# Inputs and outputs of a streaming-encoder layer laid out around the launch, with a new order at the start

## The chip, the cores and the metric

The kernel runs on one core of a Trainium2 chip, in one launch. The metric is the device time of that launch in microseconds (us). What the host does before the launch and after it (here: reshaping and transposing arrays) is no part of it.

## The reference, cut to what matters

One layer, for 1024 prompt rows and 32 sample rows (the sample has 256 cached keys and 30 rows of convolution state). Everything is float32.

```
mod = silu(c) @ w_ada + b_ada;  shift, scale, gate = split(mod, 3)
h = rms_norm(x, g_norm) * (1 + scale) + shift
q, k, v, gate_a, iq, iw, ik, glu, gate_b, merge = split(h @ w_in)
k_all, v_all, ik_all = concat([past_k, k]), concat([past_v, v]), concat([past_ik, ik])
score = sum over 8 heads of iw * relu(iq . ik_all / 8)      # the indexer
idx = top_k(score, 256 of 1024 keys; 72 of 288 for the sample)
o = softmax(q . k_all[idx] / sqrt(128)) @ v_all[idx];  y_a = (o * silu(gate_a)) @ w_a
u = ga * sigmoid(gb);  u_ext = concat([conv_state, u])
dw = depthwise conv of u_ext, width 31, + b_dw;  n = layer_norm(dw, g_ln, b_ln)
y_b = (silu(n) * silu(gate_b)) @ w_b
x = x + gate * ((sigmoid(m_a) * y_a + sigmoid(m_b) * y_b) @ w_out);  y = rms_norm(x, g_final)
outputs: y, k, v, ik and u_ext[-30:], each for the prompt and for the sample
```

## The kernel before, in words

Activations live channel by row: a tile has 128 channels on its partitions and the 1056 rows (1024 and 32) along its free axis. A matrix product in float32 is three passes of float32r: operands are split into a high and a low part, and `mm3` (lines 132 to 134) or `proj` (line 563) multiplies high by high, high by low and low by high. `proj` takes eight steps of 128 input channels; in a step it issues nine matmuls of 352 columns, and after each step it calls `step`, which takes one entry from the list `side` (transposes, indexer dots) and some convolution operations for VectorE. So whatever stands in `side` is laid between the steps of the big projections, on the same TensorE queue.

The program has a start and a long main part. The start ends when the first full projection begins. It loads the nine row tiles of x (`x:0` to `x:8`, the last being the sample; 512 KB each, six buffers), the first two thirds of `w_ada` in eight blocks of 1 MB (`a:g,h` is column group g, input half h; three buffers), the 72 columns of `w_in` for the index keys (`k`), and two blocks of 128 columns for the index queries (`q:0`, `q:1`). The loads are written in the table `LOADS` and go through SyncE's queue in that order. What the engines do with them is written in the table `ORDER`, one word per step:

- `sq`, `v`, `s`, `r`, `x`: square, variance, root, reciprocal and scaling of a row tile (the letter behind `x:i` names the engine, D VectorE, P GpSimd, A ScalarE); `t:i,h` four TensorE transposes of half a row tile into PSUM (two PSUM buffers), `c:i,h` the copy of them into `xT`.
- `m:g,h` four matmuls of `silu(c)` with a block of `w_ada`; `a:g`, `o:g`, `O:g` bring the sum of a column group into channel-by-row form and add the bias. A group serves two of the eight channel blocks.
- `h`, `i`, `l`, `S`: modulated h, its high part, its low part, and the sample's rows. Of a channel block, part `f` is rows 0 to 255, `i` 256 to 767, `t` 768 to 1023, `tf` both outer parts.
- `q:k,c` and `k:k,c`: three matmuls of channel block k for the index queries (512 or 288 columns) and index keys (352 columns). `wa`, `wd` split a weight; `b` transposes and `B` finishes the bias; `z:n` issues n matmuls on zeros that fill TensorE.

TensorE, VectorE and ScalarE run in the order written; GpSimd's queue and SyncE's after `LOADS` are ordered by the compiler. An engine waits for the instruction at the head of its queue.

In the main part the kernel transposes on TensorE what comes from the host by row and is needed by channel, or the other way: `vecs` (convolution weights, biases and state), `cache_ik` and `cache_kT` (cached keys), `nat` (k and v, which the host wants by row) and `conv_out` (the last 30 rows of u).

Of the kernel before, what the change touches and what calls it, by code (L numbers as in the profile page):

```python
# [79 lines left out]
""")  # L80
ORDER = steps("""
sq:8 z:3 b s:8 v:8 r:8 sq:3 x:8,P v:3 s:3 B sq:4 r:3 z:4 t:8,1 t:8,0 x:3,P c:8,1,D s:4 v:4 sq:5 r:4 x:4,D c:8,0,A v:5
s:5 z:4 t:4,1 r:5 t:4,0 c:4,1,A x:5,P c:4,0,D t:3,0 m:0,0 c:3,0,A sq:2 t:5,0 t:3,1 v:2 s:2 c:3,1,A r:2 c:5,0,A z:1
m:0,1 x:2,P wa:k t:5,1 a:0,D wd:k,P t:2,0 c:5,1,D sq:6 c:2,0,D z:1 t:2,1 o:0 s:6 v:6 sq:7 r:6 c:2,1,D x:6,P s:7 v:7
r:7 O:0 z:5 t:6,0 x:7,P c:6,0,A h:i,1,D z:1 m:1,0 S:0,D i:i,1 h:i,0,P i:i,0 l:i,1 t:7,0 t:7,1 c:7,0,A l:i,0 k:1,1
i:t,0 h:t,0,P c:7,1,D m:1,1 i:t,1 h:t,1,P l:t,0 k:0,1 a:1,D wa:0 k:0,2 l:t,1 o:1 wd:0,D t:6,1 sq:0 k:1,2 q:0,1 s:0
v:0 q:0,0 c:6,1,A r:0 q:1,0 O:1 x:0,P h:i,3,D i:i,2 m:2,0 h:i,2,D S:1,P i:i,3 l:i,2 t:0,0 sq:1 t:0,1 k:2,1 c:0,1,D
q:2,0 s:1 v:1 c:0,0,A r:1 q:1,1 x:1,D l:i,3 m:2,1 t:1,0 a:2,A t:1,1 c:1,0,D q:3,0 c:1,1,A h:f,0,D h:f,1,P i:tf,2
h:tf,2,D k:3,1 h:tf,3,D m:3,0 i:f,1 l:tf,2 i:tf,3 o:2 l:f,1 k:2,0 O:2 i:f,0 q:2,1 l:tf,3 i:i,4 S:2,P k:1,0 m:3,1
l:f,0 i:tf,4 h:tf,5,D i:tf,5 h:i,4,D q:3,1 h:i,5,P k:3,0 l:i,4 a:3,A k:3,2 h:tf,4,D i:i,5 k:0,0 l:tf,4 q:4,0 wa:1  # L90
l:i,5 o:3 k:4,2 O:3 k:4,0 l:tf,5 i:i,7 S:3,P q:4,1 k:5,1 h:i,7,D i:i,6 q:5,0 l:i,7 i:tf,6 k:5,2 h:i,6,D h:tf,6,P
q:5,1 i:tf,7 l:i,6 k:5,0 q:7,0 h:tf,7,P l:tf,6 k:7,1 wd:1,P q:6,0 l:tf,7 k:6,2 q:6,1 q:7,1 k:7,2 k:7,0 k:6,1 k:2,2
k:4,1 k:6,0
# [1682 lines left out]
```

## Time and profile before

| | us |
|---|---|
| median of 3 runs (1257.99 to 1259.17) | 1259.0 |
| the profiled execution | 1258.4 |
| its span, first to last instruction | 1256.6 |
| TensorE busy in the span | 1236.4 (98%) |
| VectorE, ScalarE, GpSimd busy | 894.0, 610.4, 181.4 |

The profiled execution took 1.8 us more than its span; sums are made against it. It agrees with the median to 0.6 us. Busy time of TensorE is modelled from pipelined matmuls, so a matmul's own duration (0.27 us for a small one) is longer than the time by which it holds up the next. What an instruction costs is read from the distance between starts.

### The profile page before, as it was taken

The numbers are of one execution on the slowest core, as the hardware profiler recorded it, in microseconds if no ns is written. First come the engines' busy times: TensorE is split into PE (matmuls) and PEld (weight loads), VectorE is DVE, ScalarE is ACT, GpSimd is POOL, SyncE is SP. The second block draws the span as 40 slices with busy tenths as digits, with TensorE's granted clock in tenths as the row PEclk, the third lists the DMA queues.
The fourth block names the chain that finished last, engine by engine and source line by source line (L and its number), as shares of the span: only waits on it lengthen the run. The fifth ranks groups of instructions, "written<-read, shape, count | busy, mean of one in ns | idle before, by whom it ended". The sixth has DMA issues, their size and how long they took to land.

```text
span 1256.6 us, 19134 instructions
## 1 busy us (share of the span) xinstructions
PE 1236.4 (98%) x7453; PEld 1171.9 (93%) x7453; DVE 894.0 (71%) x1416; ACT 610.4 (49%) x1128; POOL 181.4 (14%) x285
## 2 busy tenths in 40 slices
...
GB/s 314 221 51 69 73 98 59 78 69 70 102 53 53 101 52 88 67 69 78 100 98 103 171 104 47 92 203 244 39 88 89 91 105 193 207 152 180 161 88 85
DMA packets 116396, 138.49 MB, mean 110 GB/s; under 512 B 10523, under 2 KB 97843, under 8 KB 116176
## 3 DMA queue, kind: packets, MB, share of 16 engines
...
q8 instruction: 59, 0.97, 0.3%
q14 instruction: 33, 0.27, 0.1%
...
## 4 chain that ended last, share of the span: by engine, by line
PE 96%; DMA 1%; DVE 1%; ACT 1%; SPq 0%; issue 0%; POOL 0%; POOLq 0%
PE proj L563 70%; PE PT L1302 2%; PE y L132 2%; PE y L134 2%; PE y L133 2%; PE O L132 1%; PE O L134 1%; PE O L133 1%; PE misc L761 1%; PE misc L762 1%; PE misc L134 1%; PE misc L133 1%; PE misc L132 1%; DMA ada<-in_w_ada_dram 1%; PE proj L132 1%; PE proj L134 1%
## 5 line engine op out<-in xcount | busy, mean ns | idle before, releaser
L985 DVE SCALAR_TENSOR_TENSOR s<-u,vec,s 128x1086 f32<-128x1086 f32 x240 | 314.5, 1347 | 2.8
L563 PE MATMUL proj<-hh,wh 128*128 128x352 f32 x1440 | 312.1, 325 | 0.0
L563 PE MATMUL proj<-hl,wh 128*128 128x352 f32 x1440 | 311.5, 324 | 0.0
L563 PE MATMUL proj<-hh,wl 128*128 128x352 f32 x1440 | 309.1, 323 | 0.0
L563 PEld LDWEIGHTS proj<-hh,wh 128*128 128x128 f32 x1440 | 244.4, 188 | 1.8
L563 PEld LDWEIGHTS proj<-hh,wl 128*128 128x128 f32 x1440 | 246.0, 188 | 0.0
L563 PEld LDWEIGHTS proj<-hl,wh 128*128 128x128 f32 x1440 | 244.9, 188 | 0.0
L831 ACT ACTIVATE relu<-scores,cand 128x384 bf16<-128x384 f32 (+6 forms) x224 | 183.6, 821 | 72.5 <-DVE cand L846 69.9
L129 DVE TENSOR_TENSOR wl<-raw,wh 128x1024 fp32r<-128x1024 f32 (+1 forms) x82 | 97.9, 1196 | 72.1 <-ACT wh L128 72.0
L128 ACT CAST wh<-raw 128x1024 fp32r<-128x1024 f32 (+1 forms) x82 | 83.8, 1024 | 56.7 <-PE proj L563 44.6
L775 DVE SCALAR_TENSOR_TENSOR scores<-relu,iws,scores 128x384 f32<-128x384 f32 (+3 forms) x70 | 43.8, 656 | 37.2 <-ACT relu L764 36.9
L764 ACT ACTIVATE relu<-misc 128x384 f32<-128x384 f32 (+3 forms) x80 | 40.0, 523 | 58.7 <-PE misc L762 57.4
L128 ACT CAST u<-PT 128x512 fp32r<-128x512 f32 (+2 forms) x76 | 43.1, 571 | 44.8 <-PE PT L1302 42.6
L129 DVE TENSOR_TENSOR u<-PT,u 128x512 fp32r<-128x512 f32 (+2 forms) x76 | 50.6, 670 | 14.4 <-ACT u L128 14.0
L924 ACT ACTIVATE s<-proj 128x1056 f32<-128x1056 f32 x24 | 25.3, 1053 | 71.5 <-PE proj L563 71.5
L831 ACT ACTIVATION_READ_ACCUMULATOR relu<-scores,cand 128x1 f32 x224 | 41.9, 187 | 0.0
L563 PE MATMUL proj<-oa,wh 128*128 128x352 f32 x192 | 41.2, 323 | 0.0
L1282 POOL TENSOR_SCALAR E<-E,st 128x1024 f32<-128x1024 f32 (+4 forms) x36 | 33.5, 931 | 41.9 <-DVE st L1281 22.5
L563 PE MATMUL proj<-u,wh 128*128 128x352 f32 x192 | 38.5, 322 | 0.0
L1277 ACT ACTIVATE E<-E,st 128x1024 f32<-128x1024 f32 (+4 forms) x36 | 34.6, 962 | 8.0 <-DVE st L1270 7.9
...
L934 DVE TENSOR_TENSOR s<-proj,s 128x1056 fp32r<-128x1056 f32 x8 | 10.0, 1256 | 35.6 <-ACT s L932 35.6
...
## 6 DMA issues: line engine op xcount, KB each, us to landing
...
```

The lines of the kernel that those rows point to most:

```text
L128: nc.scalar.copy(hi, src)
L129: nc.vector.tensor_sub(lo, src, f32(hi))
L132: nc.tensor.matmul(out, ah, bh, start=first, stop=False)
L133: nc.tensor.matmul(out, ah, bl, start=False, stop=False)
L134: nc.tensor.matmul(out, al, bh, start=False, stop=last)
L563: nc.tensor.matmul(p[:n, c, :CH], a_[:, k, :n], b_(k, c), start=first, stop=last)
L764: nc.scalar.activation(r[:, :n], p[:, :n], AF.Relu, scale=0.125)
L775: nc.vector.scalar_tensor_tensor(acc, r[:, :n], w, acc, op0=OP.mult, op1=OP.add)
L831: nc.scalar.activation(scr[:, :s.shape[1]], s, AF.Sign, bias=f32(hold["cand"])[:, i:i + 1], accum_out=cnt[:, i:i + 1])
L985: nc.vector.scalar_tensor_tensor(d[:, :DW], u[:, k:k + DW], wj[:, k:k + 1], d[:, :DW], op0=OP.mult, op1=OP.add)
L1277: nc.scalar.activation(e, e, AF.Exp, bias=mn, scale=-1.0, accum_out=st[:, 1:2])
L1282: nc.gpsimd.tensor_scalar(e, e, st[:, 2:3], 1.0, op0=OP.mult, op1=OP.mult)
```

## The change

Arrays that the device used to rearrange are handed over rearranged, and two outputs are taken as the device has them and transposed on the host. In `LOADS` the tiles `x:0` and `x:1` stand later; `ORDER` is a new table for the start. Its functions are the same, but `b` is gone.

```diff
 LOADS = steps("""
-x:8 x:2 x:3 x:4 x:5 a:0,0 a:0,1 k x:6 x:7 a:1,0 a:1,1 q:0 x:0 a:2,0 x:1 a:2,1 a:3,0 a:3,1 q:1
+x:8 x:2 x:3 x:4 x:5 a:0,0 a:0,1 k x:6 x:7 a:1,0 a:1,1 q:0 a:2,0 a:2,1 x:0 x:1 a:3,0 a:3,1 q:1
 """)
 ORDER = steps("""
-sq:8 z:3 b s:8 v:8 r:8 sq:3 x:8,P v:3 s:3 B sq:4 r:3 z:4 t:8,1 t:8,0 x:3,P c:8,1,D s:4 v:4 sq:5 r:4 x:4,D c:8,0,A v:5
...
+sq:8 v:8 s:8 B sq:3 r:8 x:8,D s:3 sq:4 z:8 t:8,1 t:8,0 c:8,1,D v:3 c:8,0,D s:4 v:4 sq:5 r:4 x:4,D s:5 r:3 sq:2 z:5
...
-        for i in range(2):
-            c = D * i + 128 * f
-            nc.sync.dma_start(t[:, :, i], w_ada[512 * h:512 * h + 512, c:c + 128 * n].rearrange("(k p) c -> p k c", p=128))
+        nc.sync.dma_start(t, a[f"ada{g}{h}"].rearrange("p (k i c) -> p k i c", k=4, i=2))
...
-    nc.sync.dma_start(crow[0:8], fold(a["c_prompt"]))
-    nc.scalar.dma_start(crow[8:16], fold(a["c_sample"]))
-    nc.scalar.dma_start(brow[0:16], fold(a["b_ada"][:, 0:2 * D]))
-    nc.scalar.dma_start(brow[16:24], fold(a["g_norm"]))
+    nc.sync.dma_start(bc, a["cols"])
...
-            for c, c0, n in ((0, C_IK, 64), (64, C_IW, 8)):
-                nc.sync.dma_start(ikraw[:, :, c:c + n], w_in[:, c0:c0 + n].rearrange("(k p) c -> p k c", p=128))
+            nc.sync.dma_start(ikraw[:, :, :72], a["w_ik"].rearrange("p (k c) -> p k c", k=KD))
         else:
             c = 128 * i[0]
-            nc.sync.dma_start(iqraw[:, :, c:c + 128], w_in[:, C_IQ + c:C_IQ + c + 128].rearrange("(k p) c -> p k c", p=128))
+            nc.sync.dma_start(iqraw[:, :, c:c + 128], a[f"w_iq{i[0]}"].rearrange("p (k c) -> p k c", k=KD))
...
-    nc.tensor.transpose(p, crow, ident[:16, :16])
-    nc.scalar.activation(scf, p.rearrange("p (s k) -> p k s", s=2), AF.Silu)
+    nc.scalar.activation(scf, bc[:, 0:16].rearrange("p (s k) -> p k s", s=2), AF.Silu)
...
-    def vecs(q):
-        p = misc([128, 4, NR])
-        for j in range(4):
-            c = 512 * q + 128 * j
-            nc.tensor.transpose(p[:, j, :], rows[:NR, c:c + 128], ident[:NR, :NR])
-        nc.vector.tensor_copy(vec[:, 4 * q:4 * q + 4, :], p)
...
+    nc.gpsimd.dma_start(vec, a["vecs"].rearrange("p (k r) -> p k r", k=KD))
...
     def cache_ik():
-        p = misc([128, 2, 128])
-        for t in range(2):
-            nc.tensor.transpose(p[:64, t, :], cikv[:, t, :], ident)
-        pv = p[:64].rearrange("p t c -> p (t c)")
-        dup_split(pv, ikS[:, 0:PAST], ikS[:, LS:LS + PAST])
+        dup_split(cik[:64, :PAST], ikS[:, 0:PAST], ikS[:, LS:LS + PAST])
...
-    def cache_kT():
-        p = misc([128, 2, 2, 128])
-        for g in range(2):
-            for t in range(2):
-                nc.tensor.transpose(p[:, g, t, :], ck[:, 256 * t + 128 * g:256 * t + 128 * g + 128], ident)
...
     def k_done(g):
...
-            nc.gpsimd.dma_start(kt_d[128 * g:128 * g + 128, 0:TP], s[:, :TP])
-            nc.gpsimd.dma_start(kt_d[128 * g:128 * g + 128, TP + PAST:TP + LS], s[:, TP:T])
-            nat(s, g, o["k_prompt"], o["k_sample"], False)
+            nc.gpsimd.dma_start(kt_d[128 * g:128 * g + 128, :], s[:, :T])
+            nc.gpsimd.dma_start(o["kT"][128 * g:128 * g + 128, :], s[:, :T])
...
     def conv_out(j, u):
...
-            nc.tensor.transpose(p[:, 0, :], u[:, TP:TP + W - 1], ident)
-            nc.tensor.transpose(p[:, 1, :], u[:, UEXT - (W - 1):UEXT], ident)
-            nc.scalar.copy(cvo, p)
-            nc.gpsimd.dma_start(o["conv_prompt"][0, 0, :, 128 * j:128 * j + 128], cvo[:, 0])
-            nc.gpsimd.dma_start(o["conv_sample"][0, 0, :, 128 * j:128 * j + 128], cvo[:, 1])
+            nc.gpsimd.dma_start(o["convT"][128 * j:128 * j + 128, 0], u[:, TP:TP + W - 1])
+            nc.gpsimd.dma_start(o["convT"][128 * j:128 * j + 128, 1], u[:, UEXT - (W - 1):UEXT])
...
     def load_kv(g):
-        nc.sync.dma_start(raw[:, :TP + LS], kt_d[128 * g:128 * g + 128, :])
+        nc.sync.dma_start(raw[:, :TP], kt_d[128 * g:128 * g + 128, :TP])
+        nc.sync.dma_start(raw[:, TP:TP + PAST], a["kT"][128 * g:128 * g + 128, :])
+        nc.sync.dma_start(raw[:, TP + PAST:TP + LS], kt_d[128 * g:128 * g + 128, TP:T])
```

On SyncE's queue, at the program's start, these are the loads before (`xt` is a row tile of x, `ada` a block of `w_ada`, `raw` columns of `w_in`; the sizes are partitions by what each takes):

```order
L243 DMA crow<-in_c_prompt_dram 8x128
L239 DMA xt<-in_x_sample_dram 32x1024
L239 DMA xt<-in_x_prompt_dram 128x1024 x4
L235 DMA ada<-in_w_ada_dram 128x4x256 x4
L257 DMA raw<-in_w_in_dram 128x8x64
L257 DMA raw<-in_w_in_dram 128x8x8
L239 DMA xt<-in_x_prompt_dram 128x1024 x2
L235 DMA ada<-in_w_ada_dram 128x4x256 x4
L260 DMA raw<-in_w_in_dram 128x8x128
L239 DMA xt<-in_x_prompt_dram 128x1024
L235 DMA ada<-in_w_ada_dram 128x4x256 x2
L239 DMA xt<-in_x_prompt_dram 128x1024
```

And these are the loads of the same stretch now:

```order
L237 DMA bc<-in_cols_dram 128x40
L233 DMA xt<-in_x_sample_dram 32x1024
L233 DMA xt<-in_x_prompt_dram 128x1024 x4
L229 DMA ada<-in_ada_dram 128x2048 x2
L247 DMA raw<-in_w_ik_dram 128x8x72
L233 DMA xt<-in_x_prompt_dram 128x1024 x2
L229 DMA ada<-in_ada_dram 128x2048 x2
L250 DMA raw<-in_w_iq_dram 128x8x128
L229 DMA ada<-in_ada_dram 128x2048 x2
L233 DMA xt<-in_x_prompt_dram 128x1024 x2
```

A block of `w_ada` is one load of 8 KB per partition where it was two loads in rows of 1 KB; the index-key columns are one load of 2304 bytes per partition instead of rows of 256 and of 32 bytes; an index-query block has 4 KB per partition instead of rows of 512 bytes.

On TensorE, behind the last block of `w_ada` (`acc` is `m:3,1`, the last matmuls on it; `mrow` is its transposition `o:3`), stood this before:

```order
L364 MATMUL acc<-ada,scp 32x512 x4
L132 MATMUL iq_463<-hh,wh 128x288
L133 MATMUL iq_463<-hl,wh 128x288
L134 MATMUL iq_463<-hh,wl 128x288
L132 MATMUL ik<-hh,wkh 72x352
L133 MATMUL ik<-hl,wkh 72x352
L134 MATMUL ik<-hh,wkl 72x352
```

The same place now:

```order
L345 MATMUL acc<-ada,scp 32x512 x4
L132 MATMUL iq_462<-hh,wh 128x288
L133 MATMUL iq_462<-hl,wh 128x288
L134 MATMUL iq_462<-hh,wl 128x288
L331 MATMUL misc<-ident,xt 128x128 x4
L132 MATMUL ik<-hh,wkh 72x352
L133 MATMUL ik<-hl,wkh 72x352
L134 MATMUL ik<-hh,wkl 72x352
L132 MATMUL iq_447<-hh,wh 128x512
L133 MATMUL iq_447<-hl,wh 128x512
L134 MATMUL iq_447<-hh,wl 128x512
L356 MATMUL misc<-ident,mrow 128x128 x4
```

More of the index products, and a transposition of `x:1`, have moved behind the last block of `w_ada`. By the two tables, 16 key products, 9 query products and `o:3` stood behind `m:3,1` before; 17, 11, `o:3` and `t:1,1` stand there now.

On TensorE in the main part, at the value and key projections, this is a piece of the queue before (`L719` is `nat`, `L761` and `L762` are indexer dots):

```order
L719 MATMUL misc<-ident,s 128x128 x4
L761 MATMUL misc<-u,s_927 128x512
L762 MATMUL misc<-u,s_927 128x512
L563 MATMUL proj_1304<-hh,wh 128x352 x3
L563 MATMUL proj_1304<-hl,wh 128x352 x3
L563 MATMUL proj_1304<-hh,wl 128x352 x3
L761 MATMUL misc<-u,s_927 128x320
L762 MATMUL misc<-u,s_927 128x320
L719 MATMUL misc<-ident,s 128x128 x4
```

For k these transposes are gone (for v they stay, as L671), and so are L664, L672, L653, L952 and L953; nothing is put in their place on TensorE, and the entries of `side` behind them come that many steps sooner.

## Rows read from the trace of the kernel before

**Rows 1.** The page: engines, and a group (busy us, mean ns | idle before).

```profile
PE 1236.4 (98%) x7453; PEld 1171.9 (93%) x7453; DVE 894.0 (71%) x1416; ACT 610.4 (49%) x1128; POOL 181.4 (14%) x285
...
L985 DVE SCALAR_TENSOR_TENSOR s<-u,vec,s 128x1086 f32<-128x1086 f32 x240 | 314.5, 1347 | 2.8
```

**Rows 2.** Busy time by stretch: stretch, length, each engine, PEclk, DMA share, GB/s.

```profile
11.79:59.84 48.05, 44.28 (x273) 28.93 (x273) 36.14 (x82) 29.65 (x51) 26.39 (x33) 1.00 0.87 272
59.84:1240.00 1180.16, 1179.48 (x7114) 1134.72 (x7113) 848.66 (x1300) 570.02 (x1052) 146.34 (x219) 1.00 0.32 103
```

**Rows 3.** What TensorE waited for: us in total, times, longest.

```profile
PE ik L133 <- DVE hl L409: 1.5, 3, 0.6
PE acc L364 <- DMA ada<-in_w_ada_dram: 0.6, 1, 0.6
```

**Rows 4.** By stretch as rows 2: loads of x, ada, k, q:0.

```profile
6.50:8.50 2.00, 0.76 (x2) 0.00 (x0) 0.74 (x6) 1.61 (x5) 0.97 (x1) 1.00 1.02 398
10.50:13.50 3.00, 2.85 (x11) 1.72 (x9) 1.58 (x7) 1.41 (x5) 1.22 (x2) 1.00 1.09 349
15.20:16.40 1.20, 1.20 (x11) 0.29 (x4) 0.00 (x0) 1.20 (x3) 0.00 (x0) 1.00 1.13 134
26.20:27.40 1.20, 1.20 (x10) 0.36 (x10) 1.20 (x3) 0.50 (x2) 1.20 (x2) 1.00 1.22 321
```

**Rows 5.** Timeline of TensorE, the start: start us, us, engine, line, operation.

```profile
9.76 1.89 PE L464 MATMUL ik<-rest 128*128 128x512 bf16 x4
11.79 2.94 PE L350 MATMUL misc<-ident,xt 128*128 128x128 f32 x12
...
20.91 1.24 PE L464 MATMUL ik<-rest 128*128 128x512 bf16 x5
...
37.99 1.06 PE L364 MATMUL acc<-ada,scp 128*32 128x512 f32 x8 [0.61 <-DMA ada<-in_w_ada_dram]
...
44.13 1.06 PE L364 MATMUL acc<-ada,scp 128*32 128x512 f32 x8
...
49.16 0.29 PE L132 MATMUL iq<-hh,wh 128*128 128x288 f32 x1
...
49.55 0.32 PE L132 MATMUL ik<-hh,wkh 128*72 128x352 f32 x1
...
59.84 0.39 PE L132 MATMUL proj<-hh,wh 128*128 128x512 f32 x1
```

**Rows 6.** Timeline of TensorE, the main part: three places with transposes.

```profile
115.52 0.60 PE L719 MATMUL misc<-ident,s 128*128 128x128 f32 x4
115.87 0.48 PE L761 MATMUL misc<-u,s 128*128 128x512 f32 x1
116.18 0.40 PE L762 MATMUL misc<-u,s 128*128 128x512 f32 x1
116.42 0.64 PE L563 MATMUL proj<-hh,wh 128*128 128x352 f32 x3
...
128.20 0.64 PE L563 MATMUL proj<-hh,wl 128*128 128x352 f32 x3
128.77 0.46 PE L653 MATMUL misc<-ident,u 64*128 64x64 f32 x4
...
129.44 0.34 PE L762 MATMUL misc<-u,s 128*128 128x384 f32 x1
...
241.45 0.64 PE L563 MATMUL proj<-hh,wl 128*128 128x352 f32 x3
241.93 0.27 PE L952 MATMUL misc<-ident,u 128*30 128x128 f32 x1
...
242.07 0.73 PE L563 MATMUL proj<-hh,wh 128*128 128x352 f32 x3
242.63 0.65 PE L563 MATMUL proj<-hl,wh 128*128 128x352 f32 x3
```

**Rows 7.** By stretch as rows 2: the stretch in which the convolution runs.

```profile
185.00:600.00 415.00, 415.00 (x2575) 414.03 (x2575) 355.99 (x395) 263.12 (x532) 18.66 (x36) 1.00 0.23 73
```

More of the change, by code (lines that the diff above doesn't have):

```diff
@@ L85 @@
[L85 to L89, printed above, removed]
@@ L1384, in _build @@
             ("w", [(w_in, C_K, 256)], [(0, 128, k_done(0)), (128, 128, k_done(1))], 2, hrows),
-            ("call", lambda: [side.insert(2 * q, lambda q=q: vecs(q)) for q in range(2)]),
             ("w", [(w_in, C_V, 256)], [(0, 128, v_done(0)), (128, 128, v_done(1))], 2, hrows)]
@@ L1404, in _build @@
     idx_done(ikp)
-    side.extend([cache_ik, cache_kT])
+    side.append(cache_ik)
     psS_st.close()
```

91 lines of the change are left out of this document (46 added, 45 removed).

## The prediction, written before the changed kernel ran

> **What bounds the kernel now.** I read the page first: TensorE is busy for 98% of the span, VectorE for 71% [rows 1]. A share is an average, so the second view was the busy time by stretch [rows 2]. From 59.84 us, the start of the first full projection, to 1240 us TensorE is idle for 0.7 of 1180 us: there every TensorE instruction that goes is worth its distance to the next, and nothing else counts. From the first prompt transposes at 11.79 us to 59.84 us it is idle for 48.05 - 44.28 = 3.8 us. The third view, its waits, names small ones in that stretch: VectorE's low part of h for 1.5 us, a block of `w_ada` for 0.6 us [rows 3]. The fourth was the DMA rate in short stretches of the start [rows 4]: the 16 engines are busy throughout (share 1.02 to 1.22), but move 398 GB/s while tiles of x are loaded (4 KB rows), 349 GB/s in `w_ada` (1 KB rows), 321 GB/s around `q:0` (512 bytes, beside others), and 134 GB/s in the index-key columns (256 and 32 bytes). So the start has two limits close together: loads that keep coming until shortly before 44.13 us, when TensorE takes up the last block of `w_ada` [rows 5], and TensorE, which is busy from there almost to the end of the start.
>
> **The main part: transposes that go.** Cost is the distance between starts, less what the following instructions take undisturbed. All four places are on TensorE's path.
> - `nat`, four transposes: from 115.52 to 116.18 us are 0.66 us, of which the dots at 115.87 would take 0.24 (116.18 to 116.42): 0.42 us, about 0.11 each [rows 6]. For k there are four such sets: 1.7 us.
> - `conv_out`, two transposes: from 241.45 to 242.63 us are 1.18 us with two triples of `proj` of 0.48 us each (241.45 to 241.93): 0.22 us, eight times, 1.8 us [rows 6].
> - `vecs`, four transposes: from 128.20 to 129.44 us are 1.24 us, less a triple (0.48) and a dot of 384 columns (0.17, as 352 columns take 0.16): 0.59 us, twice, 1.2 us [rows 6].
> - The two sample transposes of k, two of `cache_ik` and four of `cache_kT`: eight at 0.11 us, 0.9 us, an estimate from the `nat` rows.
>
> Together 5.6 us. The lower end is 0, if another engine becomes the bound at these places (a rival below). The upper end is 48 transposes at 0.15 us, the dearest of these rows (0.59 / 4), 7.1 us.
>
> The copies from PSUM, and the stores by row, go from engines that TensorE does not wait for: nothing. The new stores of the last rows of u, 120 bytes per partition, have no row. They may hold u's buffer longer, but a buffer of u comes round after four channel blocks, and one block is 30 convolution operations of 1.347 us, 40 us [rows 1]; a store would need over 100 us to be seen. Nothing, from 0 to 0. The cached keys now enter in `load_kv` by three loads instead of one, six tiles of the `w_b` projection ahead of the first use: nothing while that cover stands. Entries of `side` come up to nine steps sooner, and what they need must be ready: the first dots follow `cache_ik` directly. Were their operands late, TensorE would wait once, for about a step of that tile (800 columns where 288 take 0.39 us [rows 5], 1.1 us); I cost it at nothing and keep the 1.1 us for the range.
>
> **The start: loads.** Up to and with the last block of `w_ada`, the amounts are from the code and the rates from [rows 4], 398 GB/s standing for the long rows of now. `w_ada`: 8.39 MB take 24.0 us at 349 and 21.1 at 398, 2.9 us less. Index keys: 0.295 MB take 2.2 us at 134 and 0.7 at 398, 1.5 less. `q:0`: 0.52 MB, 0.3 less. New in this stretch is the 0.26 MB table `vecs` on GpSimd's queue: 0.7 more. Sum 4.0 us, so the last block is there for 40.1 instead of 44.13 us. For the rows of 8 KB there is no row; from below I bound them by 349 GB/s, from above by nothing seen over 398, and I take the row that is nearest in row length, the 4 KB one.
>
> The buffers do not take it back: a block takes the buffer of the third one before it, so two further blocks lie between, 2.1 MB or 5.3 us of loading, in which four products (1.06 us [rows 5]) have to be done.
>
> **The start: TensorE.** From 44.13 to 59.84 us stood 15.7 us of work behind the last block. Now two query pieces of 288 columns (0.39 us each, 49.16 to 49.55 [rows 5]), a key product (three matmuls of 352 columns, 0.48) and a transposition (0.42) stand there in addition: 1.7 us. So the start ends at 40.1 + 15.7 + 1.7 = 57.5 us, 2.3 us sooner. The other bound: if TensorE did not wait at all after 11.79 us, it would end after 44.28 us of work less two of the eight fillers (0.25 us each [rows 5]), at 55.6 us, 4.2 us sooner. Both hold only as limits; I take 2.8, nearer to the first, since the work ahead of `m:3,1` still waits for blocks 5 to 7. The two small transposes of c and the bias, and three loads on ScalarE's queue, go from the time before 8 us, where x is waited for: nothing.
>
> **The sum**: 5.6 + 2.8 = 8.4 us from the profiled execution's 1258.4 gives 1250.0; as that lies 0.6 under the median, 1250.6 us. What a measurement can tell from no change is about 0.2%, 2.5 us.
>
> **Rival 1: the start gains nothing.** If the loads do not get faster by longer rows, the blocks arrive 1 us or so sooner (the index keys' 1.5 and `q:0`'s 0.3 less the 0.7 of `vecs`), and the 1.7 us of work moved behind the last one eat it. That leaves 5.6 us: 1253.4 us. Against it stand the 398 GB/s of the x loads in the same queue; for it, that the two rates differ also in what runs beside them. The Trainium skill ("DMA: Bandwidth & Descriptors", Bandwidth) puts a core's HBM limit at about 358 GB/s and says that this side binds for loads to SBUF. By that rule 1 KB rows were already at the limit; the trace disagrees, with 398 GB/s [rows 4], so I leave it at 17%.
>
> **Rival 2: the start gains more.** TensorE loses its waits altogether (55.6 us), and its clock rises before the prompt transposes, twelve of which took 2.94 us at 0.245 each, where 0.11 is the later price: 1.5 us more. 4.2 + 1.5 + 5.6 gives 1247.7 us. For it speaks that eight fillers now stand before any data; against, that the group-by-group dependence through ScalarE and VectorE remains (VectorE's waits in [rows 3] are of this kind). 13%.
>
> **Rival 3: the main part hides the transposes.** If VectorE or ScalarE set the pace at these places, TensorE's gain becomes a wait. VectorE is busy for 356 of 415 us in the convolution stretch [rows 7]; over the whole main part for 72% [rows 2]. TensorE's idle time is nil there, so the slack of VectorE is at least 14%, far more than the 0.22 us per channel block that go. With half of the 5.6 lost: 1253.4; with all: 1256.2. 7%, placed at 1256.
>
> **Rival 4, slower: the low clock lasts.** The granted clock reads 1.00 in every stretch [rows 2, 4], yet the fillers took 0.47 us each at 9.76 us (1.89 for four) and 0.25 at 20.91 us (1.24 for five) [rows 5]: 512 columns at the 1.2 GHz level and at the 2.4 GHz one. It rose after TensorE had worked on from 9.76 us almost without a break. Now the fillers at the head are spent at once, before data arrive, and if TensorE then works in bursts with gaps, the low level could stay. Each us spent there does half a us of work. Gain turns to loss once the rise comes 17 us later (twice 8.4), at about 33 us instead of about 15; at 40 us the time is 1250.6 + 12.5 = 1263. Against it: five more fillers stand right before the prompt transposes, and the tables have 19 in all before and now. 3%.
>
> **Chances and range.** My forecast, both parts as summed, 1249.5 to 1252, has 60%; the rivals 17, 13, 7 and 3. Faster by over 0.2% are the forecast, rivals 1 and 2 and half of rival 3: 93%; within 0.2% the rest of rival 3, 4%; slower 3%. The range of 8 in 10 takes in the ends of the two unknown costs and rivals 1 and 2: 1247.5 to 1254.5.
>
> **What the new profile would show.** The first full projection at 56 to 58 us; loads of `w_ada` at about 400 GB/s; the last block's products at about 40 us and no long wait behind them. In the main part no L653, L664, L672, L952 class of transposes, and TensorE idle for under 2 us until its tail, which keeps its length. The distance from the first full projection to the last matmul shrinks by 5.6 us. Wrong would be: a first projection after 59 us (rival 1 or 4), a sum of TensorE waits of several us in the main part (rival 3), or a tail that grew.

## The result and the profile after

| | before | after |
|---|---|---|
| median, us | 1259.1 (6 runs) | 1251.5 (6 runs, 1251.15 to 1251.74) |
| ratio | | 0.9939, interval 0.9926 to 0.9952 |
| profiled execution / its span | 1258.4 / 1256.6 | 1251.4 / 1249.6 |
| last block of `w_ada` taken up | 44.13 | 40.28 |
| first full projection | 59.84 | 57.78 |
| last matmul | 1245.77 | 1239.24 |
| main part, first projection to last matmul | 1185.93 | 1181.46 |

The kernel is 7.6 us faster; 8.4 were forecast. Of the profiled gain of 7.0 us the start gave 2.1 (forecast 2.8), the main part 4.5 (forecast 5.6), the tail behind the last matmul 0.4 (forecast nothing; why it got shorter stays open). The other 0.6 us of the 7.6 is the distance between the profiled execution before and its median, and no trace shows where it went.

The page of the kernel after, answering to [rows 1]: engines, and the convolution's group, which has not changed.

```profile
PE 1229.2 (98%) x7403; PEld 1167.6 (93%) x7403; DVE 894.1 (72%) x1413; ACT 605.2 (48%) x1115; POOL 180.6 (14%) x279
...
L931 DVE SCALAR_TENSOR_TENSOR s<-u,vec,s 128x1086 f32<-128x1086 f32 x240 | 314.3, 1346 | 2.9
```

The stretches that answer to [rows 2], the one behind the last block of `w_ada`, and the one from the fifth block to the last (length, then each engine's busy time, PEclk, DMA share, GB/s):

```profile
12.23:57.78 45.55, 42.39 (x270) 28.83 (x271) 38.09 (x86) 29.57 (x52) 31.47 (x36) 0.97 0.77 278
57.78:1233.47 1175.69, 1174.92 (x7064) 1130.93 (x7065) 846.28 (x1296) 564.73 (x1039) 142.09 (x211) 1.00 0.32 102
40.28:57.78 17.50, 16.10 (x101) 13.31 (x101) 14.93 (x24) 10.32 (x17) 14.50 (x18) 1.00 0.32 99
29.43:40.28 10.85, 10.85 (x70) 6.77 (x71) 8.92 (x27) 7.49 (x14) 7.59 (x12) 1.00 1.03 385
```

In the main part TensorE is idle for 0.8 us, as before (0.7): no wait has taken the transposes' place. What TensorE waits for in the start, answering to [rows 3] (total, times, longest):

```profile
PE misc L331 <- DVE rs_r L310: 2.9, 1, 2.9
PE misc L331 <- DVE xt L322: 2.4, 1, 2.4
PE acc L345 <- DMA ada<-in_ada_dram: 1.5, 2, 1.3
PE iq L133 <- DVE hl L390: 1.4, 1, 1.4
```

The hl wait is one wait of 1.4 us now, where there were three of at most 0.6. The DMA rates, answering to [rows 4]: x, `w_ada`, the stretch with the index keys, half a microsecond that shows the granted clock, and the whole stretch from the landing of `x:5` to that of the last block.

```profile
6.50:8.50 2.00, 1.35 (x12) 0.98 (x13) 0.80 (x2) 0.74 (x1) 0.00 (x0) 1.00 1.04 424
10.50:13.50 3.00, 1.27 (x6) 1.30 (x7) 2.44 (x12) 2.76 (x7) 0.71 (x1) 0.50 1.02 426
14.00:15.00 1.00, 1.00 (x9) 0.20 (x8) 0.96 (x4) 0.59 (x1) 1.00 (x1) 0.50 1.13 292
8.50:9.00 0.50, 0.50 (x3) 0.00 (x0) 0.06 (x1) 0.47 (x3) 0.00 (x0) 0.50 0.97 401
10.29:39.57 29.28, 25.57 (x166) 15.12 (x167) 24.09 (x67) 20.44 (x39) 16.33 (x17) 0.91 1.04 394
```

In the second row `w_ada` comes at 426 GB/s where it came at 349; over all loads up to the last block (the last row) the rate is 394. The granted clock of the second row is 0.50, the 1.2 GHz level; it fell at 8.5 us and was back at 1.00 at 15.3. The timeline of TensorE in the start, answering to [rows 5] (start us, us, engine, line, operation, idle time and releaser):

```profile
7.15 0.65 PE L331 MATMUL misc<-ident,xt 32*128 32x32 f32 x8 [2.36 <-DVE xt L322]
7.74 1.62 PE L445 MATMUL ik<-rest 128*128 128x512 bf16 x5
12.23 1.94 PE L331 MATMUL misc<-ident,xt 128*128 128x128 f32 x8 [2.88 <-DVE rs_r L310]
...
29.43 1.06 PE L345 MATMUL acc<-ada,scp 128*32 128x512 f32 x8 [1.28 <-DMA ada<-in_ada_dram]
...
40.28 1.07 PE L345 MATMUL acc<-ada,scp 128*32 128x512 f32 x8
...
54.85 0.40 PE L133 MATMUL iq<-hl,wh 128*128 128x288 f32 x1 [1.40 <-DVE hl L390]
...
57.78 0.47 PE L132 MATMUL proj<-hh,wh 128*128 128x512 f32 x1
```

The fifth block landed at 29.38, and TensorE had waited 1.28 us for it. From there it is busy without a pause for 10.85 us, up to the last block, which is taken up without a wait at 40.28 and had landed at 39.57. So the fifth block is the last load that TensorE waits for; from there on its own work sets the pace. At 54.85, near the end of the work behind it, comes the wait that was not there before. And one place of the main part, answering to the third of [rows 6]:

```profile
235.09 0.65 PE L543 MATMUL proj<-hh,wh 128*128 128x352 f32 x3
235.58 0.65 PE L543 MATMUL proj<-hl,wh 128*128 128x352 f32 x3
236.07 0.64 PE L543 MATMUL proj<-hh,wl 128*128 128x352 f32 x3
236.55 0.65 PE L543 MATMUL proj<-hh,wh 128*128 128x352 f32 x3
```

The triples follow one another at 0.48 to 0.49 us with nothing between them.

**Why the 1.4 us wait.** The timeline of VectorE and GpSimd around 51 us, after:

```profile
50.93 2.61 DVE L390 TENSOR_TENSOR hl<-h,hh 128x256 fp32r<-128x256 f32 x1 [0.30 <-POOL h L384]
50.86 2.39 POOL L439 TENSOR_TENSOR wl<-raw,wh 128x1024 fp32r<-128x1024 f32 x1
```

The subtraction of 128x256 took 2.61 us; the same shape takes 0.41 elsewhere. It began 0.07 us after a GpSimd subtraction (`wd:1`) and ended 0.29 us after that one's end: it can have got little done while GpSimd ran, and TensorE waited for its result. The Trainium skill ("SBUF — State Buffer", Who interferes with whom) says that a VectorE instruction with two SBUF inputs and a GpSimd instruction that reads SBUF cannot run together: the one that starts second is held until the first is through. The trace agrees, with these 2.61 us against 0.41.

The trace of the kernel before had such a pair in sight, on VectorE and GpSimd:

```profile
48.63 1.93 DVE L385 TENSOR_TENSOR AB<-mc,bg__182 128x8 f32<-128x8 f32 x1
...
47.94 2.60 POOL L458 TENSOR_TENSOR wl<-raw,wh 128x1024 fp32r<-128x1024 f32 x1 [0.79 <-ACT wh L453]
```

A sum of only 128x8 took 1.93 us beside the same GpSimd subtraction, and ended with it. There TensorE waited only 0.38 us behind it, one of the three small waits of [rows 3].

### The profile page after: what moved, and what is told of

The parts are those of the page before. It is cut to its first block, busy times and chain, and to the rows that moved or that the text cites. A ratio compares the mean times of both kernels' runs of the same rounds, so it can differ in the third digit from the quotient of the medians.

```text
span 1249.6 us, 18980 instructions
## 1 busy us (share of the span) xinstructions
PE 1229.2 (98%) x7403; PEld 1167.6 (93%) x7403; DVE 894.1 (72%) x1413; ACT 605.2 (48%) x1115; POOL 180.6 (14%) x279
## 4 chain that ended last, share of the span: by engine, by line
PE 96%; DMA 1%; DVE 1%; ACT 0%; POOL 0%; issue 0%; SPq 0%; POOLq 0%; ACTq 0%
PE proj L543 70%; PE PT L1250 2%; PE y L132 2%; PE y L133 2%; PE y L134 2%; PE O L132 1%; PE O L134 1%; PE O L133 1%; PE misc L712 1%; PE misc L713 1%; PE misc L134 1%; PE misc L133 1%; PE misc L132 1%; DMA ada<-in_ada_dram 1%; PE proj L132 1%; PE proj L134 1%
## 5 line engine op out<-in xcount | busy, mean ns | idle before, releaser
L857 POOL DMA_DIRECT2D mask_d<-relu x7 | 3.8, 540 | 232.1 <-ACT relu L856 232.1
```

## The experiments

Each ran beside the kernel before on the same chip, in five rounds. Times are medians in us, the other columns from its profile.

| run | time | ratio (interval) | last block | first projection | main part |
|---|---|---|---|---|---|
| after | 1251.5 | 0.9939 (0.9926 to 0.9952) | 40.28 | 57.78 | 1181.46 |
| e1_main | 1254.6 | 0.9964 (0.9951 to 0.9976) | 45.29 | 61.02 | 1181.55 |
| e2_start | 1255.6 | 0.9982 (0.9972 to 0.9992) | 39.26 | 56.76 | 1185.77 |
| e3_oldorder | 1251.3 | 0.9940 (0.9928 to 0.9953) | 42.63 | 58.31 | 1181.76 |
| e4_shortrows | 1254.6 | 0.9966 (0.9952 to 0.9979) | 43.77 | 61.27 | 1181.39 |
| e5_wd_vector | 1250.2 | 0.9935 (0.9921 to 0.9949) | 40.33 | 56.72 | 1181.39 |
| e6_onestretch | 1253.9 | 0.9958 (0.9945 to 0.9971) | 42.92 | 60.42 | 1181.46 |
| e7_fillers | 1251.5 | 0.9943 (0.9930 to 0.9956) | 40.37 | 57.88 | 1181.42 |
| e8_vecs_late | 1250.8 | 0.9937 (0.9924 to 0.9950) | 39.66 | 57.16 | 1181.51 |
| e9_stretch_wd | 1250.9 | 0.9937 (0.9924 to 0.9951) | 39.04 | 56.54 | 1181.41 |
| e10_vecs_wd | 1249.4 | 0.9925 (0.9913 to 0.9938) | 39.40 | 55.76 | 1181.40 |
| e11_all | 1249.2 | 0.9923 (0.9910 to 0.9937) | 39.62 | 56.17 | 1181.40 |
| e12_u_turn | 1249.6 | 0.9937 (0.9923 to 0.9950) | 39.40 | 55.76 | 1181.68 |

The interval of a ratio is 1.3 to 1.8 us to each side. The places come from one execution each: e2, e8 and e10, which have the same loads up to the last block, take it up within 0.4 us of one another.

### e1_main and e2_start: the two halves alone

e1 is the kernel before with the changes of the main part (`vecs`, caches, keys, conv state) and the old loads and order; e2 has the loads and the order of the start, and the old main part.

Core of e1's edit, and behind it e2's:

```diff
-    rows = uslot()
...
+    nc.gpsimd.dma_start(vec, a["vecs"].rearrange("p (k r) -> p k r", k=KD))
...
-            nat(s, g, o["k_prompt"], o["k_sample"], False)
...
-            nc.tensor.transpose(p[:, 0, :], u[:, TP:TP + W - 1], ident)
```

```diff
-x:8 x:2 x:3 x:4 x:5 a:0,0 a:0,1 k x:6 x:7 a:1,0 a:1,1 q:0 x:0 a:2,0 x:1 a:2,1 a:3,0 a:3,1 q:1
+x:8 x:2 x:3 x:4 x:5 a:0,0 a:0,1 k x:6 x:7 a:1,0 a:1,1 q:0 a:2,0 a:2,1 x:0 x:1 a:3,0 a:3,1 q:1
...
+        nc.sync.dma_start(t, a[f"ada{g}{h}"].rearrange("p (k i c) -> p k i c", k=4, i=2))
```

> The kernel before with only the changes of the main part (k, the last rows of u, the vectors and the cached keys laid out by the host; no transposes for them), its start as it was. My theory: the parts add, and TensorE's removed instructions are the main part's whole gain. The comparison of the two traces gives 4.5 us between the first full projection and the last matmul, my prediction 5.6 us: 1253.5 to 1254.6 us, first projection still at 59.8 us. Rival (the removed time turns into waits unless the start moves too): 1256 us or more.

> The kernel before with only the changes of the start (loads laid out by the host, new tables of loads and order), its main part as it was. My theory: 2.1 us from the traces, 2.8 us by my prediction: 1256.3 to 1257.0 us, first projection at about 57.8 us. Rival (the start's gain is lost again in the main part, whose TensorE queue is full): 1259 us.

They gave 4.4 and 3.4 us, together the gain of the whole. e1's time lies at the upper end of what was expected, with its first projection 1.2 us later; e2 is 0.7 us faster than expected, with its first projection 1.0 us sooner. The main part is 4.4 shorter in e1 and 0.2 in e2: the transposes' gain needs nothing of the start. In e1 the start is 1.2 us longer than before, in e2 it is 1.0 shorter than in the whole change. A load that fits this is `vecs`, which belongs to the main part's change but stands in the start; e8 below tests it.

### e3_oldorder: the loads without the order

The changed kernel with the old `LOADS` and `ORDER` (without `b`):

```diff
-x:8 x:2 x:3 x:4 x:5 a:0,0 a:0,1 k x:6 x:7 a:1,0 a:1,1 q:0 a:2,0 a:2,1 x:0 x:1 a:3,0 a:3,1 q:1
+x:8 x:2 x:3 x:4 x:5 a:0,0 a:0,1 k x:6 x:7 a:1,0 a:1,1 q:0 x:0 a:2,0 x:1 a:2,1 a:3,0 a:3,1 q:1
...
-sq:8 v:8 s:8 B sq:3 r:8 x:8,D s:3 sq:4 z:8 t:8,1 t:8,0 c:8,1,D v:3 c:8,0,D s:4 v:4 sq:5 r:4 x:4,D s:5 r:3 sq:2 z:5
+sq:8 z:3 s:8 v:8 r:8 sq:3 x:8,P v:3 s:3 B sq:4 r:3 z:4 t:8,1 t:8,0 x:3,P c:8,1,D s:4 v:4 sq:5 r:4 x:4,D c:8,0,A v:5
```

> The changed kernel with the old tables LOADS and ORDER (without the step b). My theory: faster loads carry the start, and the order only has to let them; TensorE's work behind the last block is 1.7 us less in the old order, so the start should end within 1 us of the new order's, at 57 to 59 us: 1250.7 to 1252.7 us. Rival (the new order is what gives the start's gain): first projection at 59 to 60 us and 1253.5 to 1254.5 us.

The same time as the whole change: the last block came 2.4 us later, but less work stands behind it in the old table, and the projection begins 0.5 later. The theory held. The new order as it stands is worth nothing that can be measured here; the loads are. But the new order has the 1.40 us wait in it: without that wait (e5 below) the projection begins at 56.72, 1.6 us sooner than in e3.

### e4_shortrows: the order without the long rows

```diff
-        nc.sync.dma_start(t, a[f"ada{g}{h}"].rearrange("p (k i c) -> p k i c", k=4, i=2))
+        for i in range(2):
+            c = D * i + 128 * f
+            nc.sync.dma_start(t[:, :, i], w_ada[512 * h:512 * h + 512, c:c + 128 * n].rearrange("(k p) c -> p k c", p=128))
```

> The changed kernel with the blocks of w_ada loaded from the plain matrix again, in two loads of 1 KB rows each; all else as changed. My theory: row length sets the rate (424 GB/s in 8 KB rows in the changed kernel's trace, 349 in 1 KB rows before), the last block comes 3 to 4 us later and the start ends at 60 to 61.5 us: 1253.7 to 1255.2 us. Rival 1 of the prediction (the rate does not hang on the rows): last block's products at 40 us still, 1251.5 us.

From e4's trace, the rate in the stretch that had 426 GB/s, the waits for `w_ada` and the last block:

```profile
10.50:13.50 3.00, 1.22 (x6) 1.08 (x6) 2.45 (x12) 2.92 (x7) 0.50 (x1) 1.00 1.09 353
...
PE acc L347 <- DMA ada<-in_w_ada_dram: 3.5, 3, 1.7
...
43.77 1.07 PE L347 MATMUL acc<-ada,scp 128*32 128x512 f32 x8 [0.46 <-DMA ada<-in_w_ada_dram]
```

Rows of 1 KB bring the rate back to 353 GB/s, the last block to 43.77 and 3.2 us of time. The theory held: row length (and with it two loads per block instead of one), not what runs beside it, made the difference between the two rates, and rival 1 falls. The Trainium skill ("DMA: Bandwidth & Descriptors", Bandwidth) says of the about 358 GB/s on which rival 1 drew that each core gets them with both cores of a pair streaming, and lists 425 GB/s for a single core and 16 MB; the prediction left that condition out. 426 GB/s in this stretch, with one core at work, agrees with the second figure.

### e5_wd_vector: one subtraction from GpSimd to VectorE

```diff
-k:3,0 q:7,0 h:f,0,P l:tf,6 q:6,0 wd:1,P l:f,0 k:7,1 h:tf,7,D k:6,0 l:tf,7 q:6,1 k:6,1 q:7,1 h:f,1,P k:7,0 k:7,2 l:f,1
+k:3,0 q:7,0 h:f,0,P l:tf,6 q:6,0 wd:1,D l:f,0 k:7,1 h:tf,7,D k:6,0 l:tf,7 q:6,1 k:6,1 q:7,1 h:f,1,P k:7,0 k:7,2 l:f,1
```

> The changed kernel with the low part of the second query weight (wd:1) on VectorE instead of GpSimd, at the same place of the table. In the changed kernel's trace one VectorE subtraction of 256 columns, usually 0.41 us, took 2.61 us beside this GpSimd instruction of 2.39 us, and TensorE then waited 1.40 us for a low part of h. My theory: GpSimd's long two-operand instruction holds VectorE up; without it VectorE needs 1.2 + 0.4 us for both, the wait shrinks below 0.6 us and the start ends at about 56.8 us: 1250.2 to 1250.7 us. Rival (VectorE is held up by something else, or the last index products wait for another part): the wait of 1.4 us stays, 1251.4 us.

The same place as above, in e5 (timeline of VectorE, then of TensorE):

```profile
50.63 1.41 DVE L439 TENSOR_TENSOR wl<-raw,wh 128x1024 fp32r<-128x1024 f32 x1
51.97 0.41 DVE L390 TENSOR_TENSOR hl<-h,hh 128x256 fp32r<-128x256 f32 x1
...
53.79 0.40 PE L133 MATMUL iq<-hl,wh 128*128 128x288 f32 x1 [0.29 <-DVE hl L390]
```

VectorE now does both instructions in 1.8 us, less than it took for the small one alone beside GpSimd. TensorE's wait fell from 1.40 to 0.29, and the first projection came 1.06 sooner, at the place that the theory gave. The 1.3 us of time is within its uncertainty; the fall of this wait in the trace is plain.

### e6_onestretch: a miss, and e9_stretch_wd, its cause

The index-key and index-query loads have long rows in HBM, but their tile in SBUF has a pitch of 256 columns, so each row is cut. e6 gives them one stretch per partition there too.

```diff
-            nc.sync.dma_start(ikraw[:, :, :72], a["w_ik"].rearrange("p (k c) -> p k c", k=KD))
+            nc.sync.dma_start(ikraw.rearrange("p k c -> p (k c)")[:, :72 * KD], a["w_ik"])
```

(and so for `iqraw`.)

> The changed kernel with the index-key and index-query columns landing in one stretch per partition of SBUF too (2304 bytes, 4 KB), where the changed kernel's packets for them are of 288 and 512 bytes. My theory: a transfer is cut by the shorter stretch of its two sides; the loads get 0.3 us (keys) and 0.3 us (q:0) faster, block 5 of w_ada comes 0.6 us sooner, and TensorE's wait of 1.28 us for it shrinks to 0.7: 1250.8 to 1251.2 us. Rival (packets are cut by the source alone, or the start does not hang on loads): 1251.5 us, with the same wait.

Both theories missed: e6 is 2.4 us slower than the changed kernel (the intervals of the two ratios just overlap, but the first projection comes 2.6 us later). The loads did what was wanted: between landings the keys took 0.74 us instead of 1.12, and `q:0` 1.26 instead of 1.76. The page's packet counts, of after and then of e6:

```profile
DMA packets 107898, 137.94 MB, mean 110 GB/s; under 512 B 9280, under 2 KB 88384, under 8 KB 106656
```

```profile
DMA packets 105211, 137.95 MB, mean 110 GB/s; under 512 B 8256, under 2 KB 85312, under 8 KB 103968
```

1024 packets under 512 bytes are gone (128 partitions by eight pieces of the keys, 288 bytes each), and 2048 more under 2 KB (two queries, pieces of 512 bytes). The harm is in e6's timelines of GpSimd, VectorE and TensorE, and in the granted clock (the column before DMA share):

```profile
26.28 2.36 POOL L438 TENSOR_TENSOR wl<-raw,wh 128x1024 fp32r<-128x1024 f32 x1 [1.64 <-ACT wh L433]
26.53 2.66 DVE L389 TENSOR_TENSOR hl<-h,hh 128x512 fp32r<-128x512 f32 x1
29.24 0.38 PE L133 MATMUL ik<-hl,wkh 128*72 128x352 f32 x1 [1.59 <-DVE hl L389]
30.49 1.93 PE L344 MATMUL acc<-ada,scp 128*32 128x512 f32 x8
...
30.00:32.00 2.00, 2.00 (x12) 0.53 (x12) 1.34 (x6) 0.77 (x2) 0.60 (x2) 0.63 1.05 418
32.00:34.00 2.00, 2.00 (x8) 1.26 (x5) 1.90 (x4) 2.00 (x5) 1.92 (x3) 0.52 1.03 418
```

`q:0` came sooner, GpSimd began `wd:0` 0.7 us sooner, and now ran beside a subtraction that TensorE waits for (2.66 us; 0.68 elsewhere). TensorE stood for 1.59 us, then its granted clock fell to 0.52 and eight matmuls took 1.93 us instead of 1.06. That was read off, so e9 tested it: e6 with that one instruction on VectorE.

```diff
-t:7,1 t:7,0 c:7,1,A wd:0,P k:1,1 c:7,0,A o:1 i:t,0 h:t,1,D O:1 m:2,0 i:t,1 h:t,0,D i:i,3 l:t,0 h:t,2,P q:0,0 l:t,1
+t:7,1 t:7,0 c:7,1,A wd:0,D k:1,1 c:7,0,A o:1 i:t,0 h:t,1,D O:1 m:2,0 i:t,1 h:t,0,D i:i,3 l:t,0 h:t,2,P q:0,0 l:t,1
```

> The kernel with one-stretch destinations, and wd:0 (the low part of the first index-query weight, 128x1024) on VectorE instead of GpSimd. Theory (the 2.4 us lost came from GpSimd's wd:0 lying beside VectorE's hl, which made TensorE wait 1.59 us, and from the clock that fell in that pause): no hl wait over 0.5 us before 30 us, VectorE's subtraction of 128x512 at 0.7 us throughout, the eight matmuls of m:2,0 at about 1.06 us instead of 1.93, the last block's products at 39.5 to 40.5, first full projection at 57 to 58; time 1250.6 to 1251.6. Rival (the destinations themselves cost, for example because matmul operands are read in another pitch or the loads come too soon): the products of m:2,0 stay at 1.9 us or the first projection at 60 or later; time 1253.3 to 1254.3.

The same instructions and stretch in e9:

```profile
25.50 0.68 DVE L389 TENSOR_TENSOR hl<-h,hh 128x512 fp32r<-128x512 f32 x1
26.70 1.21 DVE L438 TENSOR_TENSOR wl<-raw,wh 128x1024 fp32r<-128x1024 f32 x1
...
28.18 1.06 PE L344 MATMUL acc<-ada,scp 128*32 128x512 f32 x8 [0.62 <-DMA ada<-in_ada_dram]
...
30.00:32.00 2.00, 2.00 (x13) 1.64 (x11) 1.90 (x4) 1.35 (x4) 1.85 (x4) 1.00 1.08 436
```

At this place no instruction is stretched and the clock is 1.00; the first projection stands at 56.54 instead of 60.42, and 3.0 us of time are won. (The other pair, `wd:1` beside the last low part of h, is still there, with its 1.40 us wait.) The first theory held, and the last block and the projection came half a microsecond sooner than it said. The wait and the clock went together, so what each of them cost alone is not shown.

### e7_fillers and e8_vecs_late: what limits the start

e7 has ten more fillers ahead of the first prompt transposes; e8 loads `vecs` at the end of SyncE's `LOADS` instead of on GpSimd's queue.

```diff
-sq:8 v:8 s:8 B sq:3 r:8 x:8,D s:3 sq:4 z:8 t:8,1 t:8,0 c:8,1,D v:3 c:8,0,D s:4 v:4 sq:5 r:4 x:4,D s:5 r:3 sq:2 z:5
+sq:8 v:8 s:8 B sq:3 r:8 x:8,D s:3 sq:4 z:8 t:8,1 t:8,0 c:8,1,D v:3 c:8,0,D s:4 v:4 sq:5 r:4 x:4,D s:5 r:3 sq:2 z:15
```

```diff
-x:8 x:2 x:3 x:4 x:5 a:0,0 a:0,1 k x:6 x:7 a:1,0 a:1,1 q:0 a:2,0 a:2,1 x:0 x:1 a:3,0 a:3,1 q:1
+x:8 x:2 x:3 x:4 x:5 a:0,0 a:0,1 k x:6 x:7 a:1,0 a:1,1 q:0 a:2,0 a:2,1 x:0 x:1 a:3,0 a:3,1 q:1 w
...
+        elif op == "w":
+            nc.sync.dma_start(vec, a["vecs"].rearrange("p (k r) -> p k r", k=KD))
...
-    nc.gpsimd.dma_start(vec, a["vecs"].rearrange("p (k r) -> p k r", k=KD))
```

> The changed kernel with ten more fillers on zeros (15 for 5) ahead of the first prompt transposes, where TensorE stood idle for 2.88 us and its granted clock fell to 0.50. My theory: the clock stays up, the transposes and first products from 12.2 to 15.7 us get 1.7 us shorter, but the blocks of w_ada come no sooner, so TensorE waits longer for blocks 4 and 5 and gains under 0.5 us: 1251.0 to 1251.5 us. Rival (TensorE sets the start throughout): 1.7 us less, 1249.7 us.

> The changed kernel with the 256 KB table vecs loaded by SyncE behind the last load of LOADS instead of by GpSimd at the very start. Comparing the runs of parts: with this table in the start the first projection came 1.0 to 1.2 us later (57.78 against 56.76 us in the new start, 61.02 against 59.84 us in the old). My theory: the table takes the DMA engines from the first tiles of x: 56.8 us and 1250.3 to 1250.7 us. Rival (the differences of 1 us are scatter between executions): 1251.4 us.

From e7's timeline of TensorE:

```profile
7.92 5.10 PE L445 MATMUL ik<-rest 128*128 128x512 bf16 x15
12.86 1.04 PE L331 MATMUL misc<-ident,xt 128*128 128x128 f32 x8
...
29.52 1.07 PE L345 MATMUL acc<-ada,scp 128*32 128x512 f32 x8 [1.36 <-DMA ada<-in_ada_dram]
```

Ten more fillers kept TensorE at work. The clock did not stay up, as the theory had it: it fell at 8.9 us, but was back at 12.3 us instead of 15.3, so the first transposes took 1.04 us instead of 1.94. TensorE came to the second block 0.85 us sooner (17.50 for 18.35) and to the third at the same time as without the fillers (22.81 for 22.83), for in between it waited for VectorE and ScalarE, which prepare the next row tiles. The wait for the fifth block stayed (1.36 us for 1.28), and the projection stood at 57.88. A faster TensorE gains nothing ahead of the fifth block. e8 takes 0.26 MB from in front of all blocks: the last block and the projection came 0.62 us sooner. The rival falls, as e2, e8 and e10, all without the table there, take up the last block 0.6 to 1.0 us before the changed kernel, e5 and e7, which agree to 0.1. But 0.62 is less than the 1.0 us of the theory, and 1250.83 us lies just outside its range.

### e10_vecs_wd and e11_all: do the gains add

e10 is e8's and e5's edits together. e11 has e9's and e8's, and `wd:1` on VectorE at another place:

```diff
-k:3,0 q:7,0 h:f,0,P l:tf,6 q:6,0 wd:1,P l:f,0 k:7,1 h:tf,7,D k:6,0 l:tf,7 q:6,1 k:6,1 q:7,1 h:f,1,P k:7,0 k:7,2 l:f,1
+k:3,0 q:7,0 h:f,0,P l:tf,6 q:6,0 l:f,0 k:7,1 h:tf,7,D k:6,0 l:tf,7 q:6,1 k:6,1 q:7,1 h:f,1,P k:7,0 k:7,2 l:f,1 wd:1,D
```

> The changed kernel with vecs loaded after the other loads and wd:1 on VectorE. Theory: the two gains (1.06 us from the first projection by the missing collision, 0.6 by the load that goes) add, since one lies behind the last block of w_ada and the other before it: last block at 39.6, no hl wait over 0.5 us, first full projection at 56.1, time 1249.4 to 1249.9. Rival (both feed the same slack): first projection at 56.7, time 1250.1 to 1250.6.

> One-stretch destinations, vecs late, wd:0 on VectorE, and wd:1 on VectorE at the end of the start. Theory: if the two weights' destinations are worth the 0.9 us that index keys and queries still take above the long-row rate, the last block comes at 38.5 to 39, the first projection at 55 to 55.6, time 1248.5 to 1249.3. Rival (TensorE's work ahead of the last block sets its place now): last block at 39.5, first projection at 56, time 1249.5 to 1250.

In e10 they add: 39.40 and 55.76, no hl wait above 0.3; the 2.0 us are even 0.3 more than the two alone gave, which is within the scatter of the places. It is 9.5 us faster than the kernel before on its chip, where the changed kernel was 7.6; the intervals of the two ratios overlap, but in the traces its first projection is 2.0 us sooner at the same main part. In e11 the rival held in its places: the longer packets don't bring the last block forward any more. TensorE no longer waits for a block of `w_ada`, so its own work sets the place now. Part of that work ran at the low clock, which lasted to 17.5 us in e11 where the changed kernel has 1.00 from 15.3 us; no run has e11 with more fillers. And `wd:1` at the end of VectorE's order puts the last subtractions off, for which the first projection waits 0.7 us. Nothing was gained beyond e10.

### e12_u_turn: a theory on the main part's shortfall that fell

In the last big projection, matmuls that the change doesn't touch stand further apart. Here are two matmuls of it, the 5112th and the 5544th of the big projections (counted from 0), and the last matmul of the kernel, from TensorE's timeline before and then after:

```profile
1070.10 0.49 PE L563 MATMUL proj<-oh,wh 128*128 128x352 f32 x2
...
1141.36 0.64 PE L563 MATMUL proj<-oh,wh 128*128 128x352 f32 x3
...
1245.77 0.28 PE L134 MATMUL y<-wo15h,ml 128*128 128x256 f32 x1
```

```profile
1062.80 0.65 PE L543 MATMUL proj<-oh,wh 128*128 128x352 f32 x3
...
1134.55 0.65 PE L543 MATMUL proj<-oh,wh 128*128 128x352 f32 x3
...
1239.24 0.28 PE L134 MATMUL y<-wo15h,ml 128*128 128x256 f32 x1
```

Between the first two lie 432 matmuls of projections: 71.26 us before, 71.75 after (0.49 more). From there to the end 104.41 and 104.69 (0.28 more). It is plainest in the 72 matmuls of u with the weight's high part, 162 ns from start to start instead of 159; over all 432 the mean grew by 1.1 ns. e1 has 71.75 and e2 71.26, so it comes with the main part's change and not with the start. One buffer fewer is taken from the four that rotate under the name `u`, so I supposed that the buffers' turn sets it, and gave e10 that turn back:

```diff
+    skip = uslot()
+    nc.gpsimd.memset(skip[:, :1], 0.0)
```

> e10_vecs_wd with one more buffer taken from the four that rotate under the name u (where the kernel before took it for the rows of vecs), with one 128x1 memset in it and no other use. What it tells apart is the part of the main part's shortfall that lies in the last big projection, where the 288 matmuls on u and their neighbours stood 162 ns from start to start instead of 159 (432 matmuls from the 5112th of the big projections on: 71.75 us in all kernels with the main-part change, 71.26 in the kernel before and in the one with the start's change alone). Theory (which of the four buffers holds which channel block sets it): with the extra buffer taken the 432 matmuls are back at 71.2 to 71.3 us, the main part is 0.5 to 0.6 shorter (1180.8 us), time 1248.8. Rival (the instructions or transfers of the changed main part set it, not the buffers): 71.75 us as before, main part 1181.4, time 1249.4.

From e12's timeline:

```profile
1061.17 0.49 PE L545 MATMUL proj<-oh,wh 128*128 128x352 f32 x2
...
1132.83 0.48 PE L545 MATMUL proj<-oh,wh 128*128 128x352 f32 x2
```

71.66 us: only 0.09 of the 0.49 us came back, and the theory falls. The turn does move other matmuls by tenths (the main part is 0.3 us longer than in e10), but what makes this projection 0.7% slower stays open.

## Why the prediction was right, point by point

- **What bounds the kernel**: right for the main part, where TensorE has no slack (idle 0.8 us). Of the start it is right only in part. The prediction has the loads set the pace up to the last block of `w_ada`; in the kernel after they do so up to the fifth. e7 (a busier TensorE gains nothing ahead of it) and e4 (slower loads cost 3.5 us) show that the loads are a limit; that TensorE then works for 10.85 us without a wait, and finds the last block landed 0.7 us before, shows where it ends. The same 10.85 or 10.86 us stand in e2, e5 and e7 to e10. In the kernel before it was the sixth block: behind its wait of 0.61 us at 37.99 [rows 5] TensorE did not wait for the last one, which had landed at 43.92.
- **The main part, 5.6 us**: the mechanism was right, the size too large by 1.1 us. From the first projection to the row at 1070.10 (after: 1062.80) the gain is 5.2 us, close to the sum. `conv_out` cost 0.20 to 0.22 us at each of its eight places by the distance between the two kernels' matmuls of equal number, 1.7 in all where 1.8 was forecast; the transposes ahead of it (k's, `vecs`, caches) gave 3.3 where 3.8 was forecast; 0.2 came elsewhere. The other 0.8 us is the step that the sum did not have: it took for granted that matmuls which are not touched keep their distance, and in the last 175 us they did not (0.49 and 0.28, above). Rival 3 is refuted: no idle time took the gain, and e1 alone has it.
- **The loads, 4.0 us**: the last block landed at 39.57 instead of 43.92, 4.35 us sooner. The 398 GB/s taken for the long rows were about right: 426 is the rate of one stretch of 3 us, but from 10.29 to 39.57 us it was 394, and between landings the eight blocks took 21.3 us in all, where 21.1 was forecast. The keys took 1.12 us (forecast 0.7) and `q:0` 1.76, no less than its 0.52 MB at the 321 GB/s of before: their pieces in the tile in SBUF are of 288 and 512 bytes, and the prediction read the row's length from HBM's side alone (e6 gives 0.74 and 1.26). `vecs` cost 0.6 us (e8) to 1.2 (e1); 0.7 was forecast. These terms alone would give less than 4.0; what makes up the rest is not shown. That TensorE took up the last block at 40.28, close to the 40.1, is luck: its own work set that place, not the load.
- **TensorE behind the last block, 15.7 + 1.7 us**: 17.50 against 17.4, by two errors that cancel. Its busy time there rose by 1.4 us (16.10 from 14.68 in 15.71), not 1.7, and its idle time from 1.0 to 1.4. The small waits are gone, and one of 1.40 us for a subtraction that GpSimd held up has come. No term of the sum and no rival had that mechanism, though the trace before showed it in small. It cost 1.06 us (e5).
- **Start at 57.5**: 57.78. Against the chain's 2.3 us the prediction took 2.8 into its sum; 2.1 came. That the chain came nearer is luck too: without the unforeseen wait (e5) the start gains 3.1 us.
- **Rival 2** did not come about in the changed kernel; with two more edits (e10) the start ends at 55.76, near its 55.6, but not in its way: TensorE still waits 1.48 us for the fifth block there. **Rival 4** was seen in small: the granted clock fell to 0.50 at 8.5 us, behind the wait of 2.36 us ahead of the sample's transposes, stayed there through the wait of 2.88 us, and was back at 1.00 at 15.3 us. The first eight prompt transposes took 1.94 us for that. It cost nothing, as the loads were the limit (e7); in e6, where it fell at 30.5 us, it is part of what was lost.
